# Attention values brought back by transposes instead of a fold matmul, with the second key half converted at the end of a head pair

## The chip, the cores and the metric

The kernel runs on one core of a Trainium2 chip. A core has TensorE (PE, matmuls, with a separate row for its weight loads, PEld), VectorE (DVE), ScalarE (ACT), GpSimd (POOL), and SyncE (SP), from whose queue most DMAs are issued. Each engine works through its own instructions in order. Matrix results land in PSUM, in eight banks of 512 float32 columns; everything else is in SBUF or DRAM. The metric is the time of one execution in device microseconds; lower is better.

## The reference

One decoder layer on 1024 tokens of width 1024, in float32. A projection feeds two mixers, a dilated attention with 8 heads of 64 columns and a gated recurrence with 4 heads of 128 columns; then come the output projection, and a feed-forward part with 4096 columns. Both parts end with a norm and a residual.

```python
h = rmsnorm(x, mix_pre_norm)
q_a, k_a, v_a, q_h, f_h, i_h, g_h = split(h @ w_in)
attn = rmsnorm(dilated_mixture_attention(q_a, k_a, v_a), attn_out_norm)   # 8 heads of 64
rec  = hgrn2_recurrence(q_h, f_h, i_h, g_h)                               # 4 heads of 128
x = x + rmsnorm(concat([attn, rec]) @ w_out, mix_post_norm)
h = rmsnorm(x, mlp_pre_norm)
x = x + rmsnorm(square(relu(h @ w_ff1)) @ w_ff2, mlp_post_norm)
```

For one head, the mixture of the three dilated patterns is a softmax over one masked score matrix: `p = exp(s - max)`, `den = sum(p)`, and the output of a query is `(p @ v) / den`. That division by `den`, and the sum in `p @ v`, are what the change touches.

## The kernel before

**Precision.** Values that enter a large matmul are split into a high and a low part, and three products (high by high, high by low, low by high) are added (`three_pass`, L86 to L89). In attention, the two parts of v stand side by side: `vs` holds, for each block of 128 keys and each head, 64 columns of the high part and 64 of the low part. Keys are held likewise in `kh` and `kl`, and each is copied by DMA to the other 64 partitions, so that one matmul of 128 rows covers the high and low parts of q.

**Order of the work.** First come the recurrence heads, then the attention. The attention runs in 64 steps, 8 heads by 8 blocks of 128 queries; the 16 steps of two heads are called a pair. In step `s`, the main loop (L855 to L877) does in this order: the exponential of step s+1 (`raise_`, on ACT), the scores of step s+2 (`look`, PE, and DVE for bias and maximum), the transposes of this step's p (`turn`: one PE transpose for each key block up to the diagonal, so one in a head's first step and eight in its last; then ACT copies the high part and DVE subtracts for the low part); every second step `weigh`, and in the step after it `finish`. The scores of the next pair's first step are taken in a pair's last step but one.

**Weigh and finish.** `weigh` multiplies for two query blocks at once, with v as the stationary operand, so that PSUM holds the result with 128 rows (64 of the high part of v, 64 of the low part) and 256 query columns; ACT copies it to the SBUF tile `ot`. `finish` has to bring this back to rows of queries and add the two halves. Before, it does both with a matmul against `fold` (L620), a constant of two 64x64 identities one upon the other: one matmul for each block, with the block of `ot` as the stationary operand, into columns 256 to 383 of the same bank `po`. Then DVE scales each block by the reciprocal of its denominator, `rd`, while it reads PSUM, and writes to `anat` (L623). When a pair is complete, SP stores its `anat` to DRAM (L626); the last pair's `anat` is read directly, by the row norms (`row_norm`, L680) and by `row_gain` and `row_attn`.

**The queue of projections.** The projections of the next pair's q, v and k are a generator, `attn_proj`. After each step, `fill` takes chunks of it (three matmuls of 512 columns each) for an amount of time written by hand (3400 - 360 b ns in block b, and about 1000 to 1300 in the last twenty steps), so that PE has work while the other engines do the softmax. Each projection is done in two halves of 512 tokens, each in a bank of the tag `mm`, which has two. At the end of a half of k, DVE reads the bank and scales it by the rows' norms (`kf`, L526), ACT makes two copies of 64 rows (`kh`, L528), POOL subtracts for `kl` (L529), and SP issues four DMAs (L532, L533). The first half of the keys serves a head's first four steps, the second half is read from the fifth step on. After the last pair's projection, the queue is empty until step 48, when it gets the early output projections (`early_out`, whose rows come from `row_turn`, tiles `pmt` and `emt`, and whose weights from `w_get`, tiles `wh`, `wl`, `woh`, `wol`). `hooks` (L839 to L852) does such work after given steps.

Of the kernel before, what the change touches and what calls it, by code (L numbers as in the profile page):

```python
# [8 lines left out]
F32 = mybir.dt.float32  # L9
F32R = mybir.dt.float32r  # L10
U8 = mybir.dt.uint8
AF = mybir.ActivationFunctionType
ALU = mybir.AluOpType
AX = mybir.AxisListType
# [3 lines left out]
P = 128  # L18
# [12 lines left out]
def f32(ap):  # L31
    return ap.bitcast(F32)
# [3 lines left out]
def hymba_layer(ctx, tc, x, w_in, w_out, w_ff1, w_ff2, g_pre, lb_logits, g_mix, g_post,  # L36
                g_mlp, g_mlp_post, bias_tab, level_masks, ident_in, fold_in, out):
    nc = tc.nc
    V, S, G, TE = nc.vector, nc.scalar, nc.gpsimd, nc.tensor

    ctx.enter_context(tc.manual_schedule())
    cp = ctx.enter_context(tc.tile_pool(name="consts", bufs=1))
# [7 lines left out]
    def slab(tag, name, dtype=F32, shape=(P, T)):  # L50
        return sp.tile(list(shape), dtype, tag=tag, name=name,
                       bufs={"S": 9, "T": 9, "P": 3, "BT": 2, "V8": 2, "R": 1}[tag])
# [5 lines left out]
    def half(name, dtype=F32):  # L58
        return sp.tile([P, 512], dtype, tag="half", name=name, bufs=2)
# [2 lines left out]
        return tp.tile([P, n], F32, tag=f"c{n}", name=name)  # L62

    ident = cp.tile([P, P], F32, name="ident")
    fold = cp.tile([P, 64], F32, name="fold")
    masks = cp.tile([P, len(LEVELS), 64], U8, name="masks")
    gpre = cp.tile([P, NK], F32, name="gpre")
    lbl = cp.tile([P, HH, 2], F32, name="lbl")
# [75 lines left out]
    for h in range(HH):  # L144
        dest, box = pair_dest(f"wig{h}")
# [74 lines left out]
    rrow = slab("R", "rrow")  # L220
    mraw = slab("T", "mraw", F32, (P, len(LEVELS), 64))
    nc.sync.dma_start(out=lbl, in_=lb_logits)
    nc.sync.dma_start(out=mraw, in_=level_masks)
    nc.sync.dma_start(out=fold, in_=fold_in)

    mix_dram = dp.tile([T, D], F32, name="mixd")
    x2_dram = [dp.tile([P, D], F32, name=f"x2d{t}") for t in range(NT)]
# [232 lines left out]
    halves = ((0, 64), (64, 128))  # L460
    pairs = [None] * (AH // 2)
    first_done = [False] * (AH // 2)
    A0 = 4 * HH

    def attn_proj(pr):
        stacks = [{}, {}]
        box = [None]
        w = w_get(A0 + 3 * pr)
        for i in range(2):
            stacks[i]["q"] = slab("S", f"q{pr}_{i}", F32R)  # L470
        for hf in range(2):
            sl = slice(hf * 512, hf * 512 + 512)
            yield from proj_t(w, f"aq{pr}", hf, box)
            full = half(f"qf{pr}{hf}")
            V.scalar_tensor_tensor(full, box[0], 0.125, rrow[:, sl], op0=ALU.mult, op1=ALU.mult)
            lo = half(f"ql{pr}{hf}", F32R)
            for i, (a, b) in enumerate(halves):
                S.activation(stacks[i]["q"][a:b, sl], full[a:b], AF.Copy)
                G.tensor_tensor(out=lo[a:b], in0=full[a:b], in1=f32(stacks[i]["q"][a:b, sl]), op=ALU.subtract)
            nc.sync.dma_start(out=f32(stacks[0]["q"][64:128, sl]), in_=f32(lo[0:64]))  # L480
            nc.sync.dma_start(out=f32(stacks[1]["q"][0:64, sl]), in_=f32(lo[64:128]))
            yield 650.0
        w = w_get(A0 + 3 * pr + 1)
        vs = slab("V8", f"v{pr}", F32R, (P, NT, 2, 2, 64))
        late = None

        def v_turn(full, hf):
            pt = bank("mm", f"pvt{pr}{hf}")
            for j in range(4):
                TE.transpose(pt[:, j * P:(j + 1) * P], full[:, j * P:(j + 1) * P], ident)  # L490
            ptv = pt.rearrange("p (j h d) -> p j h d", j=4, h=2)
            dst = vs[:, hf * 4:hf * 4 + 4]
            S.activation(dst[:, :, :, 0, :], ptv, AF.Copy)
            V.tensor_tensor(out=dst[:, :, :, 1, :], in0=ptv, in1=f32(dst[:, :, :, 0, :]), op=ALU.subtract)
        for hf in range(2):
            sl = slice(hf * 512, hf * 512 + 512)
            n = 0
            for cost in proj_t(w, f"av{pr}", hf, box):
                n += 1
                if n == 4 and late is not None:  # L500
                    v_turn(*late)
                    cost += 450.0
                yield cost
            full = half(f"vf{pr}{hf}")
            V.tensor_tensor(out=full, in0=box[0], in1=rrow[:, sl], op=ALU.mult)
            late = (full, hf)
            yield 650.0
        while pr > 0 and not first_done[pr - 1]:
            yield None
        w = w_get(A0 + 3 * pr + 2)  # L510
        for i in range(2):
            stacks[i]["kh"] = slab("S", f"kh{pr}_{i}", F32R)
            stacks[i]["kl"] = slab("S", f"kl{pr}_{i}", F32R)
        for hf in range(2):
            sl = slice(hf * 512, hf * 512 + 512)
            n = 0
            for cost in proj_t(w, f"ak{pr}", hf, box):
                n += 1
                if n == 3 and hf == 0:
                    v_turn(*late)  # L520
                    cost += 450.0
                yield cost
            if hf == 0 and pr == AH // 2 - 1:
                early_rows()
            full = half(f"kf{pr}{hf}")
            V.tensor_tensor(out=full, in0=box[0], in1=rrow[:, sl], op=ALU.mult)  # L526
            for i, (a, b) in enumerate(halves):
                S.activation(stacks[i]["kh"][a:b, sl], full[a:b], AF.Copy)  # L528
                G.tensor_tensor(out=stacks[i]["kl"][a:b, sl], in0=full[a:b], in1=f32(stacks[i]["kh"][a:b, sl]),  # L529
                                op=ALU.subtract)  # L530
            for n in ("kh", "kl"):
                nc.sync.dma_start(out=f32(stacks[0][n][64:128, sl]), in_=f32(stacks[0][n][0:64, sl]))  # L532
                nc.sync.dma_start(out=f32(stacks[1][n][0:64, sl]), in_=f32(stacks[1][n][64:128, sl]))  # L533
            pairs[pr] = (stacks, vs)
            yield 650.0

    anats = [None] * (AH // 2)
    bts = {}
    stats = {}
# [42 lines left out]
    def turn(hd, b, pe):  # L582
        g, u = divmod(b, 2)
        if u == 0:
            ns = (2 * g + 5) // 4
            pts[hd, g] = [[slab("T", f"pt{q}{hd}_{g}_{s}", F32R, (P, 4, 256)) for q in "hl"] for s in range(ns)]
        for s in range((b + 4) // 4):
            nj = min(4, b + 1 - 4 * s)
            pt = bank("t", f"pt{hd}_{b}_{s}")
            for j in range(nj):  # L590
                jj = s * 4 + j
                TE.transpose(pt[:, j * P:(j + 1) * P], pe[:, jj * P:(jj + 1) * P], ident)  # L592
            src = pt[:, :nj * P].rearrange("p (j c) -> p j c", j=nj)
            hi, lo = (q[:, :nj, u * P:(u + 1) * P] for q in pts[hd, g][s])
            S.activation(hi, src, AF.Copy)  # L595
            V.tensor_tensor(out=lo, in0=src, in1=f32(hi), op=ALU.subtract)  # L596
        dn, rd = stats[hd]["dn"], stats[hd]["rd"]
        V.reciprocal(rd[:, b:b + 1], dn[:, b:b + 1])
# [16 lines left out]
    def finish(hd, g, po, ot):  # L615
        pr = hd // 2
        if anats[pr] is None:
            anats[pr] = slab("T", f"anat{pr}", F32, (P, NT, 2, 64))
        for u in range(2):
            TE.matmul(po[:, 256 + u * 64:256 + (u + 1) * 64], ot[:, u * P:(u + 1) * P], fold, start=True, stop=True)  # L620
        for u in range(2):
            b = 2 * g + u
            V.tensor_scalar(anats[pr][:, b, hd % 2], po[:, 256 + u * 64:256 + (u + 1) * 64],  # L623
                            stats[hd]["rd"][:, b:b + 1], None, op0=ALU.mult)
        if hd % 2 and g == NT // 2 - 1 and pr < AH // 2 - 1:
            nc.sync.dma_start(out=mix_dram[:, AW + pr * P:AW + (pr + 1) * P].rearrange("(n p) d -> p n d", p=P),  # L626
                              in_=anats[pr].rearrange("p n i d -> p n (i d)"))
# [183 lines left out]
    def look(s):  # L811
        if s < len(steps):
            scored[s] = score(*steps[s])
# [41 lines left out]
    for s in range(n_steps):  # L855
        if s % 16 == 6:
            first_done[s // 16] = True
        hd, b = steps[s]
        ready, to_weigh = to_weigh, []
        raise_(s + 1)  # L860
        fresh = (s + 2) % 16 == 0
        if not fresh:
            look(s + 2)
        turn(hd, b, exped.pop(s))
        if b % 2:
            to_weigh.append((hd, b // 2))
        to_fold, last_fold = [(i, g, weigh(i, g)) for i, g in ready], to_fold
        if fresh and s + 2 < n_steps:
            while pairs[(s + 2) // 16] is None:
                fill(1.0)  # L870
            if (s + 2) // 16 + 1 < AH // 2:
                drain()
                queue.append(attn_proj((s + 2) // 16 + 1))
            look(s + 2)
        for i, g, a in last_fold:
            finish(i, g, *a)
        hooks.get(s, lambda: None)()  # L877
        fill(3400.0 - 360.0 * b if s < n_steps - 20 else 1000.0 if s < n_steps - 16 else 1300.0)
# [701 lines left out]
    for t in range(NT):  # L1580
# [3 lines left out]
        for j, c in enumerate(pieces):  # L1584
            pm = banks.get(f"fe{t}{j}")
# [92 lines left out]
```

## Time and profile before

| | |
|---|---|
| median of 3 runs | 1306.63 us (1306.51 to 1308.13) |
| the profiled execution | 1308.23 us, its span 1306.4 us |
| mean granted TensorE clock | 0.992 |
| busy shares | PE 97%, PEld 83%, DVE 66%, ACT 40%, POOL 22% |
| attention steps | from about 320 to 590 us of the span |
| fold matmuls and their scaling | 337.5 to 589.2 us |

In the lines of the profile, "out<-in" names the tiles that an instruction writes and reads; the first input of a matmul is the moving one and the second the stationary one. In a group of instructions, the numbers after the bar are the busy time in us and the mean ns of one, and after the next bar the idle time of the engine just ahead of them with what ended it. In a list of waits, the numbers are the total in us, how many times, and the longest. In a timeline, a line begins with the start and the duration in us, and a bracket at its end gives the idle time ahead of it. In a table of stretches, each engine's busy time is followed by its number of instructions, and the last three numbers are the granted TensorE clock, the share of the DMA engines and GB/s.

### The profile page before, as it was taken

The page shows a single profiled execution, that of the slowest core. Times are in us where ns is not written, and L with a number is a line of the kernel's source. Part 1 is how long each engine was busy: PE and PEld are TensorE (multiplying, and loading weights), DVE is VectorE, ACT ScalarE, POOL GpSimd, SP SyncE. Part 2 cuts the span into 40 slices and gives each one's busy share as a digit, 9 for nine tenths or more (in the row PEclk, how much of TensorE's full clock was granted, in tenths as well). Part 3 has the DMA queues.
Part 4 walks back from the last instruction along what each step waited for, and adds up shares of the span by engine and source line. Part 5 has one row for each costly group of instructions (what it writes and reads, how often), then busy time and mean ns, then how long its engine had stood idle before and what let it go on. Part 6 is the DMA issues. An engine that isn't in the chain of part 4 may idle for free. (4 is left out here: it accounts for less than half of the span.)

```text
span 1306.4 us, 17483 instructions
## 1 busy us (share of the span) xinstructions
PE 1262.8 (97%) x6730; PEld 1081.0 (83%) x6730; DVE 859.5 (66%) x1427; ACT 516.9 (40%) x904; POOL 281.1 (22%) x276
## 2 busy tenths in 40 slices
PE   8999999999999999999999899999999999999997
PEld 7898989888888888887887688888877888888885
DVE  5565656575665656766758666666665776688956
ACT  6612121223555545674565422222234633444411
POOL 0000000012111112023341287665551000000011
PEclk9999999999999999999999999999999999999999
DMA  5201111122232223316252344443468554434423
GB/s 203 66 17 50 33 49 33 33 81 66 81 81 65 67 80 90 115 38 219 97 178 87 115 171 173 173 157 141 145 249 325 175 194 128 148 111 129 156 80 119
DMA packets 58724, 154.04 MB, mean 118 GB/s; under 512 B 5137, under 2 KB 13073, under 8 KB 58385
## 3 DMA queue, kind: packets, MB, share of 16 engines
q1 hardware_dynamic: 58640, 152.92, 35.1%
q8 instruction: 53, 0.87, 0.3%
q14 instruction: 31, 0.25, 0.1%
HBM read 106.77 MB, written 39.85 MB: 112 GB/s over the span
## 5 line engine op out<-in xcount | busy, mean ns | idle before, releaser
L87 PE MATMUL f<-bh,ah 128*128 128x512 f32 x392 | 152.6, 389 | 0.6 <-ACT acc L1458 0.6
L88 PE MATMUL f<-bl,ah 128*128 128x512 f32 x392 | 152.6, 389 | 0.5 <-DVE bl L84 0.5
L89 PE MATMUL f<-bh,al 128*128 128x512 f32 x392 | 152.5, 389 | 0.0
L84 DVE TENSOR_TENSOR al<-ar,ah 128x1024 fp32r<-128x1024 f32 x49 | 60.7, 1238 | 49.6 <-ACT ah L83 19.1
L87 PEld LDWEIGHTS f<-bh,ah 128*128 128x128 f32 x392 | 73.6, 188 | 16.2 <-ACT acc L1458 1.0
L88 PEld LDWEIGHTS f<-bl,ah 128*128 128x128 f32 x392 | 73.6, 188 | 16.1 <-DVE bl L84 0.8
L89 PEld LDWEIGHTS f<-bh,al 128*128 128x128 f32 x392 | 73.6, 188 | 15.3
L83 ACT ACTIVATE ah<-ar 128x1024 fp32r<-128x1024 f32 x49 | 52.3, 1067 | 52.9 <-DMA ar<-actd 27.8
L1594 POOL TENSOR_SCALAR fp<-fss 128x1 f32<-128x1 f32 x8 | 3.5, 433 | 268.9 <-ACT fd L1591 268.9
L595 ACT ACTIVATE pth<-pt 128x512 fp32r<-128x512 f32 (+2 forms) x96 | 43.4, 486 | 43.2 <-PE pt L592 42.9
L596 DVE TENSOR_TENSOR ptl<-pt,pth 128x512 fp32r<-128x512 f32 (+2 forms) x96 | 50.2, 550 | 15.1 <-ACT pth L595 15.1
L568 DVE CUSTOM_DVE_ANT_0 p<-ps,bt 128x512 f32<-128x512 f32 (+2 forms) x84 | 44.3, 552 | 23.4 <-PE ps L566 23.0
L394 PEld LDWEIGHTS pl<-qt,kt 128*128 128x128 f32 x448 | 53.1, 192 | 1.6 <-PE pm_av L89 0.9
L394 PE MATMUL pl<-qt,kt 128*128 128x64 f32 x448 | 53.2, 271 | 0.5 <-DVE qt L400 0.5
L579 ACT ACTIVATE p<-p,nm 128x128 f32<-128x128 f32 (+3 forms) x64 | 49.5, 773 | 9.3 <-DVE nm L574 6.2
L592 PE MATMUL pt<-ident,p 128*128 128x128 f32 x288 | 43.6, 279 | 7.5 <-DVE ptl L596 7.5
L529 POOL TENSOR_TENSOR kl<-kf,kh 64x512 fp32r<-64x512 f32 x16 | 20.3, 1271 | 140.2 <-ACT kh L528 139.6
L231 ACT ACTIVATE inat<-pig,rstd 128x128 f32<-128x128 f32 x32 | 11.7, 367 | 97.2 <-PE pig L89 84.1
L83 ACT ACTIVATE bh<-br 128x1024 fp32r<-128x1024 f32 x28 | 29.9, 1068 | 42.2 <-PE f L89 36.9
L79 POOL TENSOR_SCALAR ms<-hss 128x8 f32<-128x8 f32 x4 | 0.8, 198 | 209.9 <-DVE hss L446 209.9
L398 DVE TENSOR_TENSOR kt<-kt,tot 128x512 f32<-128x512 f32 x28 | 20.2, 721 | 35.7 <-PE pl L394 35.7
L592 PEld LDWEIGHTS pt<-ident,p 128*128 128x128 f32 x288 | 34.2, 143 | 11.3 <-DVE ptl L596 8.7
(1585 smaller groups left out, 3857.3 us busy)
## 6 DMA issues: line engine op xcount, KB each, us to landing
ar<-actd SPq DMA_DIRECT2D x49, 512.0 KB, 3.7
raw<-in_w_in_dram SPq DMA_DIRECT2D x28, 512.0 KB, 3.7
w1r<-in_w_ff_dram SPq DMA_DIRECT2D x14, 1024.0 KB, 6.6
br<-in_w_ff_dram SPq DMA_DIRECT2D x14, 1024.0 KB, 6.8
actd<-e SPq DMA_DIRECT2D x17, 768.0 KB, 4.2
actd<-e SPq DMA_DIRECT2D x11, 1024.0 KB, 4.1
xr<-in_x_dram SPq DMA_DIRECT2D x8, 512.0 KB, 9.3
raw<-in_w_out_dram SPq DMA_DIRECT2D x8, 512.0 KB, 3.6
```

Source lines behind the costliest of these rows:

```text
L83: S.activation(hi, src, AF.Copy)
L84: eng.tensor_tensor(out=lo, in0=src, in1=f32(hi), op=ALU.subtract)
L87: TE.matmul(dst, lhs[0], rhs[0], start=start, stop=False)
L88: TE.matmul(dst, lhs[0], rhs[1], start=False, stop=False)
L89: TE.matmul(dst, lhs[1], rhs[0], start=False, stop=stop)
L394: TE.matmul(pl[:, n * 64:(n + 1) * 64], kt[:, n * P:(n + 1) * P], qv[:, n * nb:(n + 1) * nb, 1, :], start=True, stop=True)
L529: G.tensor_tensor(out=stacks[i]["kl"][a:b, sl], in0=full[a:b], in1=f32(stacks[i]["kh"][a:b, sl]), op=ALU.subtract)
L568: V.tensor_tensor_reduce(out=pe[:, k0:k0 + n], in0=pS[:, :n], in1=bts[hd][:, o:o + n], scale=1.0, scalar=-3.0e38, op0=ALU.add, op1=ALU.max ...
L579: S.activation(pe[:, :nk], pe[:, :nk], AF.Exp, bias=nm[:, b:b + 1], accum_out=dn[:, b:b + 1])
L592: TE.transpose(pt[:, j * P:(j + 1) * P], pe[:, jj * P:(jj + 1) * P], ident)
L595: S.activation(hi, src, AF.Copy)
L596: V.tensor_tensor(out=lo, in0=src, in1=f32(hi), op=ALU.subtract)
```

## The change

`finish` now transposes each block of `ot` (128 rows, 128 queries) by PE, against the constant `ident`, into 128 columns for each block, so that the whole second half of the bank is used. DVE adds the two halves of 64 columns with one `tensor_reduce` over both blocks, reading PSUM with a stride of 64 columns between the two summands. POOL multiplies the result in place, in SBUF, by the reciprocal denominators of both blocks. The constant `fold` and its load go.

The conversion of the keys becomes a function, `keys_off`. It is called where it was for the first half of every pair and for both halves of the first pair. For the second half of the other three pairs the bank is noted in `put_off`, and the main loop calls `keys_off` just after `turn` in the next step whose block is 7, 0 or 1. The projection of these halves ends in the step with block 4 (step 12 of 16), so that the next such step is the pair's last.

```diff
-    fold = cp.tile([P, 64], F32, name="fold")
...
-    nc.sync.dma_start(out=fold, in_=fold_in)
...
+    put_off = []
+
+    def keys_off(pr, stacks, pm, hf):
+
+        sl = slice(hf * 512, hf * 512 + 512)
+        full = half(f"kf{pr}{hf}")
+        V.tensor_tensor(out=full, in0=pm, in1=rrow[:, sl], op=ALU.mult)
+        for i, (a, b) in enumerate(halves):
+            S.activation(stacks[i]["kh"][a:b, sl], full[a:b], AF.Copy)
+            G.tensor_tensor(out=stacks[i]["kl"][a:b, sl], in0=full[a:b], in1=f32(stacks[i]["kh"][a:b, sl]),
+                            op=ALU.subtract)
+        for n in ("kh", "kl"):
+            nc.sync.dma_start(out=f32(stacks[0][n][64:128, sl]), in_=f32(stacks[0][n][0:64, sl]))
+            nc.sync.dma_start(out=f32(stacks[1][n][0:64, sl]), in_=f32(stacks[1][n][64:128, sl]))
...
-            full = half(f"kf{pr}{hf}")
-            V.tensor_tensor(out=full, in0=box[0], in1=rrow[:, sl], op=ALU.mult)
...
+            if hf == 0 or pr == 0:
+                keys_off(pr, stacks, box[0], hf)
+            else:
+                put_off.append((pr, stacks, box[0], hf))
             pairs[pr] = (stacks, vs)
             yield 650.0
...
         for u in range(2):
-            TE.matmul(po[:, 256 + u * 64:256 + (u + 1) * 64], ot[:, u * P:(u + 1) * P], fold, start=True, stop=True)
-        for u in range(2):
-            b = 2 * g + u
-            V.tensor_scalar(anats[pr][:, b, hd % 2], po[:, 256 + u * 64:256 + (u + 1) * 64],
-                            stats[hd]["rd"][:, b:b + 1], None, op0=ALU.mult)
+            TE.transpose(po[:, 256 + u * P:256 + (u + 1) * P], ot[:, u * P:(u + 1) * P], ident)
+        pair = po[:, 256:].rearrange("p (u a d) -> p u a d", u=2, a=2)
+        b = slice(2 * g, 2 * g + 2)
+        dst = anats[pr][:, b, hd % 2]
+        V.tensor_reduce(dst, pair.rearrange("p u a d -> p u d a"), axis=AX.X, op=ALU.add)
+        G.tensor_tensor(out=dst, in0=dst, in1=stats[hd]["rd"][:, b].unsqueeze(2).to_broadcast([P, 2, 64]),
+                        op=ALU.mult)
...
         turn(hd, b, exped.pop(s))
+        if b in (7, 0, 1):
+            while put_off:
+                keys_off(*put_off.pop())
```

## The prediction

> **What bounds the kernel now.** I read the page's busy shares first, then the waits of PE, then the groups by line, then the timeline around the two places that the diff touches, then the granted clock there.
>
> ```profile
> PE 1262.8 (97%) x6730; PEld 1081.0 (83%) x6730; DVE 859.5 (66%) x1427; ACT 516.9 (40%) x904; POOL 281.1 (22%) x276
> PE pt L592 <- DVE ptl L596: 7.5, 3, 2.5
> PE ps L565 <- DVE mx L568: 2.7, 3, 0.9
> ```
>
> PE is busy for 97% of the span. Asked for 320 to 600 us, where the attention steps lie, the waits of PE come to 14.6 us; half of that is one wait of 2.5 us that comes three times, once in each of the first three head pairs. So PE work taken out here should shorten the span, except just ahead of a place where PE then waits for another engine.
>
> ```profile
> L620 PE MATMUL pov<-fold,ot 128*128 128x64 f32 x128 | 17.9, 263 | 0.5 <-ACT ot L612 0.5
> L592 PE MATMUL pt<-ident,p 128*128 128x128 f32 x288 | 43.6, 279 | 7.5 <-DVE ptl L596 7.5
> L623 DVE TENSOR_SCALAR anat<-pov,rd 128x64 f32<-128x64 f32 x64 | 14.6, 270 | 0.0
> ```
>
> The kernel asks for 64 fold matmuls (2 in each of 32 finishes) and the trace has 128: each runs as two passes. It asks for 288 transposes of p and the trace has 288: a transpose is one pass. The durations overlap in PE's pipeline, so the cost is read from the starts:
>
> ```profile
> 337.12 0.60 PE L592 MATMUL pt<-ident,p 128*128 128x128 f32 x4
> 337.56 0.56 PE L620 MATMUL pov<-fold,ot 128*128 128x64 f32 x4
> 337.93 0.48 PE L87 MATMUL pm_av<-hTh,wh 128*128 128x512 f32 x1
> ...
> 363.97 0.60 PE L490 MATMUL pvt<-ident,vf 128*128 128x128 f32 x4
> 364.32 0.48 PE L87 MATMUL pm_ak<-hTh,wh 128*128 128x512 f32 x1
> ```
>
> Four transposes and a finish take 0.81 us until the next projection matmul starts; four transposes alone take 0.35.
>
> ```profile
> 378.90 0.69 DVE L526 TENSOR_TENSOR kf<-pm_ak,rrow 128x512 f32<-128x512 f32 x1 [0.84 <-PE pm_ak L89]
> 379.63 1.28 ACT L528 ACTIVATE kh<-kf 64x512 fp32r<-64x512 f32 x2 [1.72 <-DVE kf L526]
> 380.94 1.04 ACT L579 ACTIVATE p<-p,nm 128x896 f32<-128x896 f32 x1
> 381.98 0.85 ACT L595 ACTIVATE pth<-pt 128x512 fp32r<-128x512 f32 x2
> 382.58 1.02 DVE L596 TENSOR_TENSOR ptl<-pt,pth 128x512 fp32r<-128x512 f32 x2 [1.52 <-ACT pth L595]
> 383.33 0.98 PE L592 MATMUL pt<-ident,p 128*128 128x128 f32 x7 [2.50 <-DVE ptl L596]
> ```
>
> This is the repeated wait. The second key half is converted (kf on DVE, two copies on ACT) after the pair's step with five transposes; ACT then does the exponential of 896 columns, the split of the six transposes, and only then does PE get a bank for the next seven. No projection is left in the queue for PE to do meanwhile.
>
> **The change, part by part.**
>
> *Fold to transposes.* Transposes go at 0.107 us each: (0.35 - 0.03)/3, with 0.03 from one transpose to the projection matmul after it (324.59 to 324.62). Six in a row are 0.03 + 5 x 0.107 = 0.565 instead of 0.81: 0.245 saved per finish, 7.8 us over 32. Not all is kept. Ahead of the three 2.5 us waits the finish lies within the wait; ahead of the three 0.9 us waits (341.86 and its two likes, behind a DVE weight split) it only lengthens the wait; and three finishes after the third pair's wait (525 to 534 us) stand in front of waits for the output weights. That leaves 32 - 9 = 23, or 5.6 us; ends 3.3 (ten more lost) and 7.8.
>
> *Scaling.* On DVE two scalings from PSUM, 0.46 us together where they stand in the timeline, give way to one reduce of 256 elements from PSUM with a stride. No row has it. Between the scaling (64 elements, 270 ns) and the reduce of L446 (512 elements from SBUF, 684 ns) the slope is 0.92 ns, so 0.45 us; ends 0.27 and 0.68 (as slow as 512). I take 0.45, the interpolation: no change for DVE. At the upper end the nine places where DVE is late lose 9 x 0.22 = 2 us. POOL is given 32 multiplies of 128x128. L688 has that shape, 459 ns, so 15 us more on an engine 22% busy. Behind a multiply wait ql and kl subtractions and the row statistics of the last steps, and SP's store of anat. The reader of anat that comes soonest is ACT's square of the first row (568.85, already waiting 0.51 for DVE), late by about 0.5; ACT has idle gaps of 0.2 to 1.3 us in the steps after, so nothing for the end. A multiply that overlaps a DVE operation with two SBUF inputs slows it: the weight split took 2.03 us (339.16) beside ql on POOL and 1.23 otherwise. Only weight splits are of that kind here, and they seldom stand beside a finish: 0, at most 1 us. The load of fold (0.33 us of SP's issue at 12.0, landing unwaited) goes: 0.
>
> *Keys put off.* With kf and the two copies gone from here, ACT could start the 896-column exponential at 377.91, where the copy of ot ends (its maximum is ready at 377.11), and be through by 379.2. The split of the six transposes then waits for them alone: 379.62 + 0.63, the lag that 387.42 to 388.05 shows, is 380.25 rather than 381.98. DVE's scores are through at about 380.9, so ptl starts 1.6 us earlier than 382.58 and so do the seven transposes. The wait does not vanish: the rest is 0.9, and 1.1 with the shorter finish. In the first two pairs: 2 x 1.6 = 3.2 us, ends 0 and 5.
>
> In its new place, the step with eight transposes, the bundle is one DVE operation (0.69), two ACT copies (1.28), two POOL subtractions (2.6) and four DMAs on SP. In the first two pairs a new query projection is queued there. DVE is free from 391.7 to 395.5 and ACT from 393.1 to 396.2, so what queues behind (exponential at 389.02, split at 390.79, both about 3 us later) still meets the two transposes at 396.38. The held bank is read by about 390.9; the projection that wants it starts at 395. The last subtraction ends near 394.1 and lands 0.5 + 2.2 later, 396.8; the first score that reads second-half keys is at 400.95. What SP issues next behind those DMAs is q's copy at 398.32. Cost 0 while these covers of about 4 us last.
>
> *Third pair.* Its wait also slowed PE afterwards:
>
> ```profile
> 515.00:518.00 3.00, 0.89 (x9) 0.75 (x7) 1.44 (x6) 2.95 (x7) 2.52 (x2) 1.00 0.44 102
> 518.00:520.00 2.00, 1.60 (x8) 1.60 (x9) 1.11 (x5) 1.47 (x3) 1.92 (x3) 0.58 0.47 109
> 520.00:522.00 2.00, 2.00 (x13) 2.00 (x12) 1.23 (x3) 0.64 (x2) 2.00 (x3) 0.57 0.03 8
> ```
>
> The granted clock (the number after POOL's) fell to 0.58. Seven transposes took 1.40 us instead of 0.74 and nine of the following matmuls 0.21 each instead of 0.12: about 1.6 us. A shorter wait may keep the clock up. But no projection is queued at this pair's end. The bundle lands between the eight transposes (522.61) and the first early output matmuls (528.00), in front of ACT's and DVE's splits of emt (525.51, 526.14) and the second output weight (526.00, 527.09): 0.69 + 1.28 = 2.0 us that PE soon waits for. SP's load of the next output weight (528.34) comes behind the last keys' copy, which POOL (from about 526.7, 2 x 1.3) lets go at 529.3: 1.0 late, within the 2.0 by which the buffer that it needs comes free later anyway. Net 1.6 + 1.6 - 2.0 = 1.2; I take 1.0, ends -2.0 and 3.2.
>
> **Sum.** 5.6 + 3.2 + 1.0 = 9.8 us. The profiled execution took 1308.23 (span 1306.4), 1.6 above the median 1306.63. Against its own time that is 1298.4; against the median 1296.8, which I give as 1297.
>
> **Rivals.**
>
> 1. *The wait only moves.* PE waits for the keys wherever they are converted: at the step with eight transposes, DVE and ACT are as loaded. For it: that is my own reading of the third pair. Against: two query-projection chunks (385.74) lie between in the other two. Then 5.6 - 2.0 = 3.6: 1303. Chance 0.14.
> 2. *More goes than counted.* All three 2.5 us waits vanish and the clock holds: 7.8 + 7.5 + 1.6 = 16.9, less up to 2 for the third pair: 1291. Against: ptl still needs pth and DVE's scores. Chance 0.10.
> 3. *PE's clock drops.* More transposes and fewer matmuls could bring stretches like 518 to 522 at every pair's end: 3 x 1.6 = 4.8 dearer, 1302. Against: at 386 to 390 eight transposes ran at clock 1.00. Chance 0.05. The Trainium skill, "TensorE: Matmul & The Clock Gate", Part 4, says that a transpose doesn't count as PE activity for the clock gate as a matmul does; by that rule this case would come true, and the row at 386 to 390 doesn't show it.
> 4. *DVE takes the gain back.* A reduce of 0.68 or more, and two-input operations slowed by POOL, eat about 8 us (32 x 0.22 + 1, all of it shown in the end): 1305, within the bound. Chance 0.07. The Trainium skill, "GPSIMD Engine Reference", 1. Specifications, says that the SBUF interfaces are shared, with contention for DVE instructions that have two SBUF inputs; the weight split's 2.03 against 1.23 agrees.
> 5. *Slower: the keys come too late.* Where the fifth step of the next pair scores the second half (400.95), PE stands until they land. The cover is 4.1 us; each us beyond costs 3. To undo 9.8 and go 2.6 beyond, landing would have to slip by 4.1 + 12.4/3 = 8.2 us, which takes POOL or SP blocked behind something not in the trace. About 1310. Chance 0.07.
>
> **How the numbers follow.** My forecast has the remaining 0.57, from 1293 to 1301. Faster by over 0.2% (2.6 us, about what a measurement of this kernel can tell from no change) are the forecast and rivals 1 to 3: 0.86. Same is rival 4: 0.07. Slower is rival 5: 0.07. The range goes from beyond rival 2 (1290) to between rivals 1 and 4 (1304.0); rivals 4, 5 and a little of 2 stay out.
>
> **What would show it.** Right: no fold row; 64 transposes at the finish; six transposes to a projection matmul in about 0.57 us; the reduce near 0.45; PE's waits for ptl at about 1.0 us twice instead of 2.5; clock near 1.00 at the third pair's end, with new PE waits for emt or the output weights after it. Wrong: a new PE wait for kh, kl or the bank; a reduce above 0.7; PE waiting for ptl at the pairs' first steps; a granted clock below before's 0.992.

## The result, and the profile after

The changed kernel takes 1298.62 us (median of 4 runs, 1296.25 to 1299.66); the kernel before, beside it, 1306.9 us (4 runs). By these medians it is 8.3 us faster. The ratio over the runs of the batch is 0.9927, with an interval of 0.9914 to 0.994, which is 9.5 us, give or take 1.7. Its profiled execution took 1296.25 us (span 1294.4, granted clock 0.993). In a further batch on another chip, given below, the same two kernels stood at 0.992 (0.9907 to 0.9933).

The page's busy shares of the changed kernel, then those of its waits of PE from 315 to 600 us that the text takes up (total, times, longest):

```profile
PE 1254.5 (97%) x6666; PEld 1071.5 (83%) x6666; DVE 857.5 (66%) x1395; ACT 515.6 (40%) x904; POOL 295.5 (23%) x308
```

```profile
PE ps L573 <- DVE mx L576: 3.5, 3, 1.2
PE pt L600 <- DVE ptl L604: 3.4, 6, 1.0
PE pwe L86 <- ACT woh L82: 1.4, 1, 1.4
PE pmt L718 <- DVE emt L83: 1.0, 1, 1.0
PE pwe L87 <- DVE wol L83: 0.8, 1, 0.8
```

PE has 64 instructions and 8.3 us of busy time less, DVE 2.0 us less, POOL 14.4 more. The wait for `ptl` was 7.5 us in three; it is now three of about 1.0 and three new ones of 0.2. The wait for `mx` grew from 0.9 to 1.2 each. At the last pair's end the wait for `woh` is longer (1.4, before it was 0.9), the one for `emt` is new, and the one for `wol` is as it was (0.8).

The finish and the former 2.5 us wait, in the timeline of the changed kernel (start, duration, and in brackets the idle time ahead):

```profile
335.91 0.60 PE L600 MATMUL pt<-ident,p 128*128 128x128 f32 x4
336.35 0.38 PE L628 MATMUL pov<-ident,ot 128*128 128x128 f32 x2
336.49 0.48 PE L86 MATMUL pm_av<-hTh,wh 128*128 128x512 f32 x1
...
375.89 1.03 ACT L587 ACTIVATE p<-p,nm 128x896 f32<-128x896 f32 x1
378.36 0.87 ACT L603 ACTIVATE pth<-pt 128x512 fp32r<-128x512 f32 x2 [1.34 <-PE pt L600]
378.99 1.02 DVE L604 TENSOR_TENSOR ptl<-pt,pth 128x512 fp32r<-128x512 f32 x2
379.74 0.98 PE L600 MATMUL pt<-ident,p 128*128 128x128 f32 x7 [0.97 <-DVE ptl L604]
```

Four transposes and a finish take 0.58 us until the next projection matmul, where they took 0.81. The exponential of 896 columns is over before the six transposes start, so the split of them waits for PE alone, and PE for 0.97 us instead of 2.50.

To see where the time went I cut the spans at PE's own marks: the first transpose of the attention, the rows of six, seven and eight transposes at the ends of the first three pairs, the first early output matmul (`pwe`), the first matmul of the rest of the output projection (`pwo`) and the first feed-forward matmul (`f115a`). Two profiles of each kernel, the second of each from the experiments below, in us:

| stretch | before | before again | after | after again | difference of the means |
|---|---|---|---|---|---|
| start to attention | 324.6 | 324.1 | 323.4 | 324.0 | -0.7 |
| to the first six | 55.0 | 55.0 | 54.3 | 54.3 | -0.7 |
| six to seven, three pairs | 11.1 | 11.1 | 6.1 | 6.0 | -5.1 |
| seven to the next six, two pairs | 127.6 | 127.6 | 125.1 | 125.2 | -2.5 |
| third seven to eight | 4.2 | 4.2 | 2.7 | 2.7 | -1.5 |
| third eight to `pwe` | 5.4 | 5.4 | 6.6 | 6.6 | +1.2 |
| `pwe` to `pwo` | 59.3 | 57.5 | 59.2 | 59.5 | +1.0 |
| `pwo` to `f115a` | 377.2 | 378.3 | 376.7 | 377.6 | -0.6 |
| `f115a` to the end | 341.9 | 341.8 | 340.3 | 340.3 | -1.5 |

From the start of attention to `pwo`, where the change works, the gain is 7.6 us. Another 1.5 comes from the very end of the kernel, which the change doesn't touch; that is taken up with the last experiment. The start and `pwo` to `f115a` differ as much between two profiles of one kernel as between the kernels.

A part of the differences is the granted clock, which falls to 0.50 for pieces of 3.4 us. From the start of attention to `pwo`, before has two such pieces (at 518.3 and 535.4 us), before again one (517.6), the two profiles of the change one each (526.6 and 528.2). One piece costs 1.5 to 1.7 us, an estimate from two pairs of stretches: `pwe` to `pwo` takes 59.28 us in before, with a piece, and 57.54 in before again, without; and with the fold alone (below) a seven to the next six takes 64.15 us with a piece, at 447.5, and 62.59 without.

### The profile page after: what moved, and what is told of

Its sections match the earlier page's. It is cut to its first block, busy times and chain, and to the rows that moved or that the text cites. A ratio compares the mean times of both kernels' runs of the same rounds, so it can differ in the third digit from the quotient of the medians.

```text
span 1294.4 us, 17367 instructions
## 1 busy us (share of the span) xinstructions
PE 1254.5 (97%) x6666; PEld 1071.5 (83%) x6666; DVE 857.5 (66%) x1395; ACT 515.6 (40%) x904; POOL 295.5 (23%) x308
## 5 line engine op out<-in xcount | busy, mean ns | idle before, releaser
L633 POOL TENSOR_TENSOR anat<-anat,rd 128x128 f32<-128x128 f32 x32 | 14.5, 455 | 140.4 <-DVE anat L632 136.6
L1127 POOL TENSOR_TENSOR e<-x,e 128x512 f32<-128x512 f32 x14 | 20.7, 1476 | 102.0 <-DVE x L1078 102.0
```

Of the source, the lines that this page charges most:

```text
L1127: eng[0].tensor_tensor(out=e1[:, 3], in0=a21, in1=e1[:, 2], op=ALU.add)
```

## The experiments

Each is compared with the kernel before on the same chip, run in turn with it. The first four share one chip, the next four another, the next three a third; the last has a fourth.

**The changed kernel again.** No edit.

> The changed kernel once more, as the yardstick for the others. The profile pair says: 4.8 us from the finish (PE marks outside the waits move 0.7, 1.3, 1.2 and 1.6 us together), 3 x 1.7 from the waits for ptl at the pairs' ends, 1.5 from the clock behind the third of them, minus 2.7 given back between the third pair's eight transposes and the fourth step of the last pair: 8.7 us. Expected about 8.5 us below the kernel before; the 1.2 us that the profile shows ahead of the attention should not come back as a part of the change.

Measured 1297.34 us (1297.0 to 1298.67), ratio 0.992 (0.9907 to 0.9933): 10.8 us by the medians and 10.5 by the ratio, where 8.5 was expected. The following runs stand against it, those on other chips by their ratios.

**The fold alone.** The keys stay where they were; only `finish` is new.

```diff
-            if hf == 0 or pr == 0:
+            if True:
                 keys_off(pr, stacks, box[0], hf)
```

> Transposes, reduce and POOL multiply as in the changed kernel, all keys converted where they were before. My theory (the two parts add): 4.8 us below the kernel before, three waits of about 2.7 us for ptl, the low clock behind the third still there. Rival (the finish's saving is eaten by the next wait, the keys bring all): within 1.5 us of the kernel before.

Measured 1300.41 us (1299.14 to 1302.93), ratio 0.9942 (0.9929 to 0.9955): 7.7 faster than before, more than expected. The wait for `ptl` is back, 0.16 us longer each time, and the three short ones of 0.2 stay:

```profile
PE pt L600 <- DVE ptl L604: 8.5, 6, 2.7
```

By the marks, the attention up to `pwo` takes 257.9 us, 3.9 less than before's mean of 261.8; that is near the 4.8 that was expected. Its profile has two pieces of slow clock there (447.5 and 515.7), before's have two and one. The rest of the 7.7 lies elsewhere.

**The keys alone.** The keys are put off as in the change; `fold`, its matmuls and the scaling on DVE are those of before.

```diff
-            TE.transpose(po[:, 256 + u * P:256 + (u + 1) * P], ot[:, u * P:(u + 1) * P], ident)
...
+            TE.matmul(po[:, 256 + u * 64:256 + (u + 1) * 64], ot[:, u * P:(u + 1) * P], fold, start=True, stop=True)
...
+            V.tensor_scalar(anats[pr][:, b, hd % 2], po[:, 256 + u * 64:256 + (u + 1) * 64],
+                            stats[hd]["rd"][:, b:b + 1], None, op0=ALU.mult)
```

> Fold matmul and DVE scaling as before, the second key halves put off as in the changed kernel. My theory: 5.1 + 1.5 - 2.7 = 3.9 us below the kernel before, waits for ptl about 0.8 us. Rival (the keys bring all): 7 to 8 us below. Rival (the wait only moves): within 1 us of the kernel before.

Measured 1301.01 us (1298.9 to 1303.09), ratio 0.9946 (0.9932 to 0.996): 7.1 faster, again more than expected. The wait for `ptl` is 0.8 us three times, and six to seven takes 2.0 us as in the changed kernel. So the shorter wait is the keys' doing, and the rest of it doesn't depend on the fold. The time alone is what the rival (the keys bring all) had asked for, 7 to 8 us; against it stand the fold's own 7.7 and the marks, by which this kernel gains 2.6 up to `pwo`.

By medians the two parts alone sum to 14.9 us, and the whole gave 10.8 in that batch (before 1308.15). Something is counted twice; the last experiment finds 1.5 us of it.

**The last pair's keys not put off.**

```diff
-            if hf == 0 or pr == 0:
+            if hf == 0 or pr in (0, AH // 2 - 1):
```

> As the changed kernel, but the last pair's second key half is converted where it was before. My theory: it loses 1.7 of the wait and 1.5 of the clock and wins 2.7 back: 0.5 us slower than the changed kernel, about nothing. Rival (putting off the last pair's half costs more than it brings, since no projection is queued there): 1 to 2 us faster than the changed kernel. Rival (it is the best of the three, because of the clock): 3 us slower.

Measured 1295.98 us (1293.19 to 1298.6), ratio 0.9911 (0.9893 to 0.9929). The expectation was half a microsecond slower than the change; it is 1.4 faster in the median, with overlapping intervals. Its six runs form two groups, 1293.2 to 1293.8 with a granted clock of 0.996 over the span and 1298.1 to 1298.6 with 0.991. The profile is of the first group. It has the 2.66 us wait at the third pair's end back, and yet the clock holds behind it; in the fold-alone kernel the same wait is followed by a slow stretch. In the stretches behind that wait (bounds, length, busy time of PE, PEld, DVE, ACT and POOL, then the granted clock, the DMA share and GB/s), the fold alone and then this kernel:

```profile
515.00:518.00 3.00, 2.75 (x15) 2.76 (x16) 2.14 (x7) 1.96 (x4) 1.94 (x3) 0.62 0.28 64
```

```profile
510.00:513.00 3.00, 2.46 (x22) 2.47 (x23) 2.34 (x7) 2.15 (x6) 1.80 (x4) 1.00 0.36 83
```

So a wait of 2.5 to 2.7 us can be followed by a slow clock, but need not be. From `pwe` to `pwo` this kernel takes 55.9 us, the fold alone 56.1, and the changed kernel 59.2 and 59.5. Of that difference of over 3 us, up to 1.7 is the piece of slow clock that both profiles of the changed kernel have there and these two haven't; the rest, 1.5 to 1.8, and 1.2 more ahead of `pwe`, is what keeping the last pair's keys early saves. It costs 1.7 at the wait. All this is read from an execution of the faster group; the other three runs, 5 us slower, have no profile.

**The multiply on DVE.** POOL is left out of the finish.

```diff
-        G.tensor_tensor(out=dst, in0=dst, in1=stats[hd]["rd"][:, b].unsqueeze(2).to_broadcast([P, 2, 64]),
+        V.tensor_tensor(out=dst, in0=dst, in1=stats[hd]["rd"][:, b].unsqueeze(2).to_broadcast([P, 2, 64]),
```

> As the changed kernel, but the multiply by rd is done by DVE in place. By the nearest row (128x128 with two SBUF inputs, 0.34 us) DVE gets 32 x 0.3 = 9 us more. My theory (DVE's idle time hides it but for the nine places where it is late): 1 to 3 us slower than the changed kernel. Rival (the hop to POOL delays the readers of anat and slows DVE's two-input operations): 1 us faster. Rival (DVE has no room): 6 us slower or more.

Measured 1296.27 us (1296.16 to 1297.49), ratio 0.9912 (0.9896 to 0.9929): no slower than the change. DVE had 9.9 us more to do (867.4 against 857.5) and none of it is seen in the end.

**The reduce issued twice.** The same sum is written a second time, so the result is the same.

```diff
         V.tensor_reduce(dst, pair.rearrange("p u a d -> p u d a"), axis=AX.X, op=ALU.add)
+        V.tensor_reduce(dst, pair.rearrange("p u a d -> p u d a"), axis=AX.X, op=ALU.add)
```

> As the changed kernel, but the reduce is issued twice, so that DVE gets 32 x 0.36 = 11.5 us more where rival 4 of the prediction placed it. My theory: 2 to 4 us slower than the changed kernel. Rival (a slower reduce takes the whole gain): 8 to 11 us slower.

Measured 1296.94 us (1296.18 to 1298.73), ratio 0.992 (0.9905 to 0.9934): nothing, with 13.2 us more on DVE. The tile views of the two kernels (duration in ns: least, median, most) show what DVE did, the multiply in the first and the second reduce in the second:

```profile
L633 DVE TENSOR_TENSOR anat<-anat,rd x32: 291/293/680, 343.5 to 580.6; 128x128 f32<-128x128 f32 x32
```

```profile
L633 DVE TENSOR_REDUCE anat<-pov x32: 424/425/426, 342.0 to 579.9; 128x128 f32<-128x256 f32 x32
```

With these two runs the choice between DVE and POOL for the scaling, and the reduce's size up to twice its own, are out as terms of the sum.

**The keys two steps later still.** The put-off halves are converted in the second step of the next pair.

```diff
-        if b in (7, 0, 1):
+        if b == 1:
```

> As the changed kernel, but the put-off key halves are converted in the next pair's second step. Worked out from the changed kernel's profile: kf at about 395.2, the copies to 397.2, the subtractions to 399.2, landing at about 401.9, needed at 396.88: PE stands for 5 us in each of the first two pairs and about 3 in the third: 11 to 13 us slower than the changed kernel, and slower than the kernel before. Rival (the landing of the keys has more room than it seems): within 2 us of the changed kernel.

Measured 1312.4 us (1311.09 to 1313.42), ratio 1.0038 (1.0026 to 1.005): slower than before, some 15 us slower than the change. PE waits for the keys:

```profile
PE ps L573 <- DMA kh<-kh: 3.7, 3, 1.4
PE ps L574 <- DMA kl<-kl: 2.6, 3, 1.1
```

Neither line exists in the changed kernel. The expectation was 11 to 13 us slower than it. Between the two steps lies the whole cover. In the first pair, the copy of `kl` that the first reader needs is issued at 389.21 us in the changed kernel and at 398.68 here, 9.5 later. The copies take 2.2 us to land, and the changed kernel's first score on the second half is at 396.88: 5.5 us of cover, of which 9.5 leaves 4.0 uncovered. By the marks each of the first two pairs takes 3.9 us longer, apart from a piece of slow clock at 401.3; 0.8 of it is a new wait for `qf`. Rival 5's rate of 3 per us would make 12 of it. At the last pair's end the first output weight is 2.8 us late in the same kernel, and the clock fell to 0.50 between 535 and 540, which makes the rest.

**The last pair's keys one step later.** In the changed kernel the third pair's bundle stands between the last transposes and the first output matmuls. Here it is done in the next pair's first step.

```diff
-        if b in (7, 0, 1):
+        if b == (0 if s > 46 else 7):
```

> As the changed kernel, but the last pair's second half is converted one step later (step 48, behind its single transpose), where ACT stands 2.5 us for the load of an output weight. My theory: emt and the second output weight come 2 us sooner, the landing of the keys is just in time: 1 us faster than the changed kernel (2 faster to 1 slower). Rival (the chain of output weight loads sets this stretch, wherever the bundle is): no difference.

Measured 1295.83 us (1294.99 to 1296.44), ratio 0.9909 (0.9894 to 0.9923): 1.4 below the changed kernel's ratio, with overlapping intervals. The waits for `woh`, `wol` and `emt` at that place are gone, and PE waits 2.9 us ahead of `pmt` with nothing but its own issue named. By the marks, the 1.2 us ahead of `pwe` are saved, and `pwe` to `pwo` takes 59.4, as in the changed kernel. So the stall has moved, and most of its length with it.

**Something to do in the rest of the waits.** To the edit above comes a new amount for `fill`, so that in the first three pairs a projection chunk (three matmuls) is left for the time between the six and the seven transposes.

```diff
-        fill(3400.0 - 360.0 * b if s < n_steps - 20 else 1000.0 if s < n_steps - 16 else 1300.0)
+        fill(20.0 if s % 16 == 12 and s < n_steps - 16 else 900.0 if s == 43 else
+             3400.0 - 360.0 * b if s < n_steps - 20 else 1000.0 if s < n_steps - 16 else 1300.0)
```

> As the run with the last pair's half at step 48, and two projection chunks are held back from a pair's step 12 to step 13 (in the last pair to steps 45 to 47), so that PE has work where it waited 1.0 us for ptl. My theory: the three waits of 1.0 go, and in the last pair 1 to 2 us more of waiting and with it the clock's fall: 3 to 5 us faster than the changed kernel. Rival (the chunks only push the chain of DVE and ACT back by their own length): no difference.

Measured 1291.8 us (1291.0 to 1294.73), ratio 0.9882 (0.9868 to 0.9896), 5 us below the changed kernel's ratio: as expected, at the upper end. Of these, 3.5 lie between this run and the one before. The three waits of 1.0 are gone, the three of 0.2 stay:

```profile
PE ps L573 <- DVE mx L576: 3.5, 3, 1.2
PE pt L600 <- DVE ptl L604: 0.5, 3, 0.2
```

**And the late weight split later.** The first line above shows what is left: DVE's maximum is late because a split of 1024 columns, 2.03 us beside a POOL subtraction, stands ahead of it (at 337.95 in the changed kernel). Here the split of the keys' weights is asked for five chunks into the projection of v instead of at its start.

```diff
-        w = w_get(A0 + 3 * pr + 1)
+        w = parts[A0 + 3 * pr + 1] if pr else w_get(A0 + 1)
...
+                if n == 5 and late is None:
+                    w_get(A0 + 3 * pr + 1)
```

> As the run before, and the split of the next projection weight is issued five chunks later in the v projection, away from POOL's ql, so that DVE's split takes 1.2 us instead of 2.0 and the scores ahead of PE's 1.2 us waits aren't behind it. My theory: these three waits shrink to 0.4 or less, 2 to 3 us faster than the run before. Rival (the split has only moved in front of another score): no difference.

Measured 1288.1 us (1287.27 to 1291.01), ratio 0.9854 (0.9838 to 0.987), 3.7 us faster than the one before it (2 to 3 were expected; the intervals just overlap) and 19 faster than the kernel before all changes. The waits for `mx` are gone. The split itself now stands behind the reduce that begins at 339.40, at 339.72, and takes 1.21 us, with no subtraction on POOL beside it:

```profile
339.72 1.21 DVE L83 TENSOR_TENSOR wl<-raw,wh 128x1024 fp32r<-128x1024 f32 x1
```

This is the best version here; it beats both kernels.

**The transposes of the finish twice.** They write the same columns again, so that the result is the same.

```diff
-        for u in range(2):
+        for u in (0, 1, 0, 1):
```

> As the changed kernel, but the two transposes of each finish are issued twice: 32 x 0.214 = 6.8 us more PE work at the very place where the fold matmul went. My theory (a finish's PE time shows, but for the places ahead of a wait): 4 to 5.5 us slower than the changed kernel. Rival (what happens in the finish shows in full): 7 us. Rival (it is hidden, and the finish's saving came from somewhere else): 1 us or less.

Measured 1299.63 us (1298.14 to 1304.22), ratio 0.9944 (0.9928 to 0.9959): 3.1 us slower than the change by the ratios, with intervals that just overlap, and less than the 4 to 5.5 expected. By the marks up to `pwo` it is 2.1, or about 3.8 without the piece of slow clock that both profiles of the change have there and this one hasn't. The 64 transposes are 6.8 us of PE's time at 0.107. Part of it came back as shorter waits: three for `ptl` of 0.8 in place of six that summed to 3.4, and 0.9 instead of 1.2 for `mx`. So about half of what a finish costs PE is seen in the end. The clock didn't suffer: 1.00 from 510 to 550 us in its profile, 0.995 over its span. The Trainium skill, "TensorE: Matmul & The Clock Gate", Part 4, would let one expect a lower clock from more transposes; this run doesn't show it.

**The kernel before again.**

> The kernel before once more, to see how much of the difference between the two first profiles lies outside the attention. In the first profile of before, attention began at 324.6 us and the part behind the first feed-forward matmul took 341.9 us; in all eleven profiles of other versions they are 323.1 to 324.7 and 340.1 to 340.5. If that is a matter of the execution, this profile shows about 340.1 to 340.5 for the last part. If it belongs to the kernel (both parts of the change would then take it away, which would explain why their gains together exceed the whole's), it shows 341.9 again, within 0.3. By the first theory the stretch from the start of attention to the first feed-forward matmul is 639.9 again, give or take 1.5; where the clock falls around 515 to 540 us may differ. The ratio to before is 1.000 within 0.0015.

Measured 1307.08 us (1304.94 to 1312.92), ratio 1.0002 (0.9987 to 1.0018). The part behind `f115a` takes 341.8 us, so the first theory fell: the 1.5 us belong to the kernel. (In the twelve profiles of other versions this part took 339.8 to 340.6, a little wider than the expectation has it.) They lie in two places, the same in both profiles of before. ACT waits for a load of activations 0.7 us longer than in the changed kernel (8.29 and 8.31 against 7.63), and PE waits 0.6 for ACT in turn (`acc`, L1458), which it doesn't in the changed kernel; lines of ACT in the profile of before again and of after:

```profile
1003.45 1.06 ACT L83 ACTIVATE ah<-ar 128x1024 fp32r<-128x1024 f32 x1 [8.31 <-DMA ar<-actd]
```

```profile
993.69 1.06 ACT L82 ACTIVATE ah<-ar 128x1024 fp32r<-128x1024 f32 x1 [7.63 <-DMA ar<-actd]
```

And the span ends 4.1 to 4.2 us after the last output DMA is issued, against 3.3. With either part of the change alone, both are already as in the changed kernel (waits of 7.70 and 7.66, ends after 3.2 and 3.1). That is why the parts sum to more than the whole by 1.5 us. What in the two programs makes these transfers differ was not tried and stays open. The other 2.6 of the excess of 4.1 is not settled: three ratios with half-widths of about 1.7 us each go into it. By the marks up to `pwo` there is no excess at all: 3.9 for the fold and 2.6 for the keys, against 7.6 for both. But the profiles differ in their pieces of slow clock (the keys alone have two, from 528.7). With about 1.6 us taken off for each it would be 4.7 and 3.5 against 6.8, an estimate from one or two profiles of each: an excess of 1.4 us, which lies in the last pair (below).

## Why the prediction was right, point by point

The forecast was 9.8 us against the profiled execution's own time, 1297 against the median. Measured by the medians were 8.3 and, in the later batch, 10.8; by the ratios 9.5 and 10.5. The time and the direction are right, and so are the mechanisms of nearly every step. But 1.5 us of the measured gain was not in the sum, and the terms behind the 9.8 came to 7.6: what the last pair gives back was put too low, and the finishes were counted too high. That the total came so near to 9.8 is in part luck.

**Fold to transposes: forecast 5.6, measured 3.2 up to the third pair's six transposes, and not seen behind them.** The size of one was right: 0.23 instead of 0.245 per finish. The count was too high. Of the 23 finishes counted, 16 lie ahead of the third pair's six transposes, 3.9 us; the marks there show 0.7 + 2.5 = 3.2, three finishes before the first wait and five in each of the next two stretches. The other seven, 1.7 us, are in the last stretches; there the fold alone gains about 1.4 and the whole change nothing (worked out under the third pair). The finish ahead of the `mx` wait only lengthened it, from 0.9 to 1.2, as the prediction has it. (The lower end of this term, with ten more finishes lost, is 3.2 by the prediction's own numbers and not 3.3.) Missed were the new waits of 0.2 us for `ptl`: PE, being faster, now arrives ahead of DVE at a place in each pair where it had just been late. They are in the list of waits as the three short ones of six.

**Scaling: forecast 0, measured 0.** The reduce was taken at 0.45 from an interpolation; it takes 0.405. The multiply was taken at 459 ns from another row of that shape; its median is 399 and its mean 455. From the tile view of `anat` in the changed kernel:

```profile
L632 DVE TENSOR_REDUCE anat<-pov x32: 404/405/417, 341.8 to 579.6; 128x128 f32<-128x256 f32 x32
L633 POOL TENSOR_TENSOR anat<-anat,rd x32: 398/399/1309, 342.3 to 580.1; 128x128 f32<-128x128 f32 x32
```

Of the ends, the lower was nearer for the duration, and it didn't matter: a second reduce of 425 ns per finish cost nothing either. The nine places where DVE is late didn't lose by it, which the prediction had allowed for with up to 2 us. Two multiplies of some 1.3 us stand out; one, at 518.44, lies beside DVE's split of `wol`.

**Keys put off: forecast 1.6 each, measured 1.7.** In all three pairs the seven transposes start 1.7 us earlier after the six, and the rest of the wait is 0.97 where 0.9 to 1.1 was forecast. The steps named for it are in the timeline shown above one by one. The new place costs nothing, as forecast:

```profile
386.49 0.67 DVE L469 TENSOR_TENSOR kf<-pm_ak,rrow 128x512 f32<-128x512 f32 x1
390.57 0.46 SPq L476 DMA_DIRECT2D kl<-kl  x1
396.88 0.22 PE L573 MATMUL ps<-kh,q 128*128 128x128 f32 x1
```

The last of the copies lands 2.2 us after its issue, 4.1 ahead of the first score, the cover that the prediction gives. In fact the first score reads the stack whose copy was issued at 389.21, so that the true cover is 5.5.

**Third pair: forecast 1.6 and 1.6 less 2.0, measured 1.7 and 1.5 less about 2.7 and a slow clock.** The shorter wait and the seven transposes at full clock came as forecast. What is given back was mis-sized. The places were right: `emt` and `woh`, first in the timeline of before, then in the changed kernel's:

```profile
527.09 1.23 DVE L84 TENSOR_TENSOR wol<-raw,woh 128x1024 fp32r<-128x1024 f32 x1 [0.25 <-ACT woh L83]
528.34 0.35 SPq L104 DMA_DIRECT2D raw<-in_w_out_dram  x1
532.29 1.06 ACT L83 ACTIVATE woh<-raw 128x1024 fp32r<-128x1024 f32 x1 [1.56 <-DMA raw<-in_w_out_dram]
```

```profile
516.97 0.69 DVE L83 TENSOR_TENSOR emt<-pmt,emt 128x512 fp32r<-128x512 f32 x1 [1.64 <-ACT emt L82]
518.05 1.40 DVE L83 TENSOR_TENSOR wol<-raw,woh 128x1024 fp32r<-128x1024 f32 x1 [0.39 <-ACT woh L82]
519.48 0.72 SPq L103 DMA_DIRECT2D raw<-in_w_out_dram  x1
523.85 1.06 ACT L82 ACTIVATE woh<-raw 128x1024 fp32r<-128x1024 f32 x1 [2.50 <-DMA raw<-in_w_out_dram]
```

By SP's list of waits, its load of the next output weight waits for `wol`'s split, and it follows that split's end by 0.02 to 0.03 us in both kernels. The last keys' copy is issued at 518.39, 1.1 us ahead of the load, and doesn't set it, so the cover that the prediction gave for it was there. But the split itself comes later behind the keys, and takes 1.40 us instead of 1.23 beside a multiply on POOL. The load is now issued 1.3 us behind the first `pwe`, where it was 0.3; ACT's wait for it grows from 1.56 to 2.50, and PE's wait for ACT from 0.9 to 1.4. Then comes what the prediction hoped to be rid of:

```profile
522.00:525.00 3.00, 1.37 (x8) 0.92 (x8) 1.65 (x8) 1.15 (x2) 0.40 (x1) 1.00 0.99 363
525.00:530.00 5.00, 4.24 (x17) 3.61 (x18) 3.38 (x9) 1.79 (x5) 0.00 (x0) 0.66 1.02 352
```

PE is busy for 1.37 of 3 us, and in the next 5 us the clock is 0.66 in the mean. Before also had such a stretch, 0.66 from 535 to 540 us, in one of its two profiles. By the table this part gives back 1.2 ahead of `pwe`. Behind it, `pwe` to `pwo` rose by 1.0 in the mean of two profiles. With 1.7 taken off for each piece of slow clock (an estimate), the stretch takes 57.6 and 57.5 in before, 57.5 and 57.8 in the change, 57.7 with the keys alone and 56.1 with the fold alone. So the clock makes up most of the rise. The finishes gain some 1.4 there, by the one profile of the fold alone, and the put-off keys take that away again. They give back about 1.2 + 1.5 = 2.7, not 2.0, so that in the last pair putting them off hardly pays.

**The sum.** From the start of attention to `pwo` the table has 3.2 + 5.1 + 1.5 - 1.2 - 1.0 = 7.6. In the terms of the forecast: the 16 finishes brought 3.2 instead of 3.9; the keys of the first two pairs 3.4 instead of 3.2; the third pair, with the seven finishes behind it, 1.0 instead of 1.0 + 1.7 = 2.7. The largest miss is the last. The 1.5 at the end of the kernel is in none of the steps, and it made up for most of what was missing.

**The rivals.** The first (the wait only moves) is refuted for the first two pairs, where nothing came in its place, and true in part for the third. The second (all goes) needed something for PE to do in the wait: the change doesn't bring it, the `fill` edit does, and it is worth 3.5 us. The third (clock) is not seen: 1.00 at the first two pair ends, and 1.00 with twice the transposes. The fourth (DVE) is refuted by the two runs that load DVE further. The fifth (keys too late) is a true mechanism, shown by the run two steps later, with a cover of 5.5 us where I put 4.1.

**Misses in the experiments' expectations.** Both parts alone were forecast too small, by the end of the kernel and by what isn't settled; the last pair's early keys were expected to cost and did not; DVE's extra work was expected to cost 1 to 4 us and cost none; the keys two steps later cost some 15 us where 11 to 13 were expected; the doubled transposes cost 3.1 by the ratios where 4 to 5.5 were expected.

## What to carry to other kernels

A wait for an engine is often not that engine's work but what stands ahead of it in an in-order queue. Moving three operations from a step without filler work to one with it took 1.7 us out of a 2.5 us wait, and more edits of that kind (the last keys a step later, a chunk of matmuls kept back for the wait, a weight split put behind the softmax) gave 8.6 us more by the ratios. When an engine becomes faster, look for the places where it now arrives early: three waits of 0.2 us took back a part of the gain that no list of existing waits could show. Compare stretches of two profiles only after counting the pieces of slow clock in each. And run the kernel before twice with a profile before you add parts up: here 1.5 us of the difference lay in a stretch that the change doesn't touch, and either part alone brought all of it.

## What the runs showed of the hardware that was not expected

The granted clock falls in pieces. In all fourteen profiles, each recorded fall but the last, which runs into the end of the span, lasts 3.4 us, or twice or three times that, at 0.50; a stretch that holds only a part of one shows a mean such as 0.66. In the 3.4 us ahead of it PE was idle for at least 0.9 us: 0.95 ahead of the fall at 137.5 us of the changed kernel, 2.18 ahead of that at 526.6, 2.41 ahead of that at 518.3 in before. But it doesn't fall each time, nor in each execution of one program. After the 2.5 us wait for `ptl` it fell in the third pair in both profiles of before and not in the first two; with the fold alone it fell in the second and the third. The same kernel with the same waits had it at 535.4 us in one profile and not in the other. One kernel's runs fall into two groups 5 us apart, with clocks of 0.996 and 0.991 over the span. What decides it stays open.

POOL and DVE hinder each other in both directions. DVE's weight split took 1.21 us alone and 2.03 beside a POOL subtraction. A POOL multiply of 128x128 took 0.40 us alone and 1.25 where it started just after such a split, as at 339.94 in the best version, and there the split kept its 1.21. The Trainium skill, "GPSIMD Engine Reference", 1. Specifications, has this contention for DVE instructions with two SBUF inputs; these rows agree, and show that POOL can be the one that pays.
